# Moving the gate projections of five token tiles from a branch-B unit to the branch-A unit after it

## The chip, the cores and the metric

The kernel runs on one core of one Trainium2 chip. The metric is the device time of one launch in microseconds (us). Before the change three runs took 2355.49 to 2356.97 us, with a median of 2356.01. Engines are called by the profile's names: PE is TensorE, DVE is VectorE, ACT is ScalarE, POOL is GpSimd, and SP is SyncE, which issues nearly all DMAs.

## What is computed

One layer of a streaming encoder: 2048 prompt tokens, and 8 running streams with 16 new tokens each and a cache of 512. The parts that matter here:

```
h = rms_norm(x, norm_g) * (1 + scale) + shift
qa, ka, va, za, qb, kb, vb, zb, ga, gb = split(h @ w_in)
# branch A: 4 heads, two softmaxes each, chunk-causal
w = softmax(q1 k1) - lam * softmax(q2 k2);  oa = w @ v
# branch B: 8 heads, stick-breaking, causal
a = sigmoid(z) * prod over later keys of sigmoid(-z);  ob = a @ v
ya = (norm(oa) * silu(za)) @ w_branch_a;  yb = (ob * silu(zb)) @ w_branch_b
y = x + gate * ((sigmoid(ga) * ya + sigmoid(gb) * yb) @ w_out)
```

The change is about `ga` and `gb`, each 1024 columns wide: the gates. They are projected from h like q, k and v, but nothing reads them before the last stage of the kernel.

## The kernel before

**Tiles and units.** Tokens go in 17 tiles of 128: prompt tiles 0 to 15, and tile NT = 16 with the 8 x 16 new tokens of the running streams. Attention goes in 8 units. Unit u = 2h is head h of branch A, unit u = 2h + 1 is a pair of heads of branch B. Values that need more than 16 bits are held as two float16 parts, so that a projection of 1024 input rows is 8 x 3 = 24 matmuls (high by high, high by low, low by high) of up to 512 columns.

**Projections.** `project(U, t)` (L406) makes q, k, v and z of one unit for one tile: 12 pieces of two matmuls each (L427) into one bank of PSUM ("mm"), then evictions, rotation and stores. For units with a gate width, 12 more pieces follow (`gate_piece`, L487): 24 matmuls of 512 columns (L494) into the one bank "t" from the same tile of h, an eviction with a scale on ACT (L497) into one half of the buffer gts, and a store to `g_d` in memory (L498). `GATES` (L58) gives the units their columns: branch-A units have width 0, each of the four branch-B units has 512 of the 2048 gate columns. So all 17 tiles' gates of a branch-B unit are projected in the same step as its q, k, v and z.

**Weights.** `prepare_unit(u)` (L307) loads the weights of a unit, takes their norm, and cuts them into float16 parts, in buffers from the list `free`: 4 buffers for q, k, v and z, and 4 more for the gates of a branch-B unit. It begins in the attention step of tile NT of the unit before (for unit 1: of tile 3), and is spread over the following steps. `begin` (L842) gives all buffers of the unit before back to the list when the projections of the next unit start.

**The order of the work.** All projection pieces stand in one list, `line`, in order of steps (u, t), t = NT, 0, 1, ..., 15. The transposes of q and k of a step (`transpose_qk`, L502), also through bank "t", follow behind piece 5 of the next step. The outer loop goes through the steps' attention: scores (L629, L630, and the mask L633), then for branch A the row maximum with the eviction (L548), exponentials (L119), sums and weights (L586 to L593), and for branch B two sigmoids (L119), a scan along the keys (L606), a product on POOL (L612) and the float16 parts (L562, L563); DMA turns the weights into `wt` (L570); two steps later come the products with v (L677 to L679, L681 and L682). At each attention step `take` (L878) takes projection pieces from the line up to `position(len(steps) * past / whole + LEAD)`, where `past` is a planned duration of the attention so far (`duration`, L888) and LEAD is 5 steps. So projections run five tiles ahead at the start of a unit, and the first five tiles of a unit are projected beside the last attention tiles of the unit before. `interleave` (L91) mixes these pieces evenly among the score pieces and the products with v; a scheduler then settles each engine's order. Each engine works through its own queue in that order.

**The last stage** (from L1250) reads `g_d`, z and the attention's output tile by tile, makes the branch products, and with them the output; the cached streams' attention is done beside it.

Of the kernel before, what the change touches and what calls it, by code (L numbers as in the profile page):

```python
# [20 lines left out]
AF = mybir.ActivationFunctionType  # L21
# [6 lines left out]
KT = D // P  # L28
# [4 lines left out]
NT = SEQ // P  # L33
# [22 lines left out]
SAMPLE_TIME = 0.3  # L56

GATES = [(u // 2 * 512, u % 2 * 512) for u in range(8)]  # L58

C_ROPE = 0  # L60
C_ID = C_ROPE + 17 * 96
# [48 lines left out]
def layer_kernel(ctx: ExitStack, tc: tile.TileContext, a: dict):  # L110
    nc = tc.nc
    V, S, G, T = nc.vector, nc.scalar, nc.gpsimd, nc.tensor
# [61 lines left out]
    def buffers_of_4k(name, n):  # L174
        pool = ctx.enter_context(tc.tile_pool(name=name, bufs=1, side="right", reuse_waits="tile"))
        return [pool.tile([P, 1024], F32, name=f"{name}{i}") for i in range(n)]


    free = buffers_of_4k("wa", 8)
# [7 lines left out]
    def bank(tag, dt=F32):  # L187
        return ps.tile([P, 512 if dt == F32 else 1024], dt, tag=tag, name=f"ps_{tag}", bufs=BANKS[tag])
# [19 lines left out]
    def total(col, n=1):  # L208

        p = bank("t")  # L210
        T.matmul(p[:, 0:n], ones, col, start=True, stop=True)
        return p[:, 0:n]

    def scales(square, pool, name, n=1):

        tag = "sc" if n == 1 else f"sc{n}"
        kw = {} if n == 1 else dict(bufs=1)
        q = tiny.tile([P, n], F32, tag=tag + "_q", name="sc_q", **kw)
        V.tensor_scalar(out=q, in0=square, scalar1=2.0 ** -46, scalar2=None, op0=ALU.max)
        f = tiny.tile([P, n], I32, tag=tag + "_f", name="sc_f", **kw)  # L220
        V.tensor_scalar(out=f, in0=q.bitcast(I32), scalar1=24, scalar2=None, op0=ALU.logical_shift_right)
        e = tiny.tile([P, 2 * n], I32, tag=tag + "_e", name="sc_e", **kw)
        V.tensor_scalar(out=e[:, 0:n], in0=f, scalar1=-1.0, scalar2=204.0, op0=ALU.mult, op1=ALU.add)
        V.tensor_scalar(out=e[:, n : 2 * n], in0=f, scalar1=50.0, scalar2=None, op0=ALU.add)
        s = pool.tile([P, 2 * n], I32, tag=name, name=name)
        V.tensor_scalar(out=s, in0=e, scalar1=23, scalar2=None, op0=ALU.logical_shift_left)
        return s.bitcast(F32)
# [39 lines left out]
    def sum_squares(src, n, dst, width=1024, scale=1.0):  # L267

        for i in range(0, n, width):
            junk = tiny.tile([P, width], F16, tag="junk", name="junk", bufs=1)  # L270
            w = min(width, n - i)
            S.activation(out=junk[:, 0:w], in_=src[:, i : i + w], func=AF.Square, scale=scale,  # L272
                         accum_out=dst[:, i // width : i // width + 1])

    def add_up(acc, n):
        if n == 1:
            return acc[:, 0:1]
        col = tiny.tile([P, 1], F32, tag="col", name="col")
        V.tensor_reduce(out=col, in_=acc[:, 0:n], axis=AX.X, op=ALU.add)
        return col  # L280
# [6 lines left out]
    def split(hi, lo, src, s, on=None):  # L287

        if on is S:
            S.activation(out=hi, in_=src, func=AF.Identity, scale=s)  # L290
        elif on is G:
            G.tensor_scalar(out=hi, in0=src, scalar1=s, scalar2=0.0, op0=ALU.mult, op1=ALU.add)
        else:
            V.tensor_scalar(out=hi, in0=src, scalar1=s, scalar2=None, op0=ALU.mult)
        V.scalar_tensor_tensor(out=lo, in0=src, scalar=s, in1=hi, op0=ALU.mult, op1=ALU.subtract)
# [8 lines left out]
    sh_box = []  # L304
    units = [None] * 8

    def prepare_unit(u, keep=None):  # L307


        h, kind = u // 2, u % 2  # L310
        U = dict(h=h, kind=kind, u=u, w=[], wg=[], bufs=[])
        units[u] = U
        raw = {}
        g0, gw = GATES[u]
        gk = 1024 // gw if gw else 0

        def fetch(name, k):
            raw[name, k] = b = free.pop(0) if keep is None else keep[:, k // 2, :]
            if name == "w":
                st = b.rearrange("p (k j n) -> p k j n", k=2, n=P)  # L320
                for i in range(2):
                    load(out=st[:, i, :, :], in_=w_in[:, k + i, :].rearrange("p (j n) -> p j n", n=512)[:, 4 * kind : 4 * kind + 4, h * P : (h + 1) * P])
            else:
                load(out=b.rearrange("p (k n) -> p k n", k=gk), in_=w_in[:, k : k + gk, 4096 + g0 : 4096 + g0 + gw])

        def norm(name, k, i):
            if k == 0:
                U[name + "acc"] = unit.tile([P, 4], F32, tag=name + "acc", name=name + "acc")
            fetch(name, k)
            sum_squares(raw[name, k], 1024, U[name + "acc"][:, i : i + 1])  # L330

        def bounds():
            fsq = total(add_up(U["wacc"], 4))
            U["sw"] = scales(fsq, unit, "sw")
            U["fsq"] = unit.tile([P, 1], F32, tag="fsq", name="fsq")
            V.tensor_copy(out=U["fsq"], in_=fsq)

        def bounds_g():
            U["sg"] = scales(total(add_up(U["gacc"], KT // gk)), unit, "sg")

        def split_to(name, k):

            b = free.pop(0)
            U["bufs"].append(b)
            if keep is None:
                free.append(raw[name, k])
            return raw[name, k], b.bitcast(F16)

        def cut(k):
            st, w = split_to("w", k)  # L350
            for i in range(2):
                x = w.rearrange("p (i f n) -> p i f n", i=2, f=2)[:, i, :, :]
                split(x[:, 0, :], x[:, 1, :], st[:, i * 512 : (i + 1) * 512], U["sw"][:, 0:1], S if i % 2 else G)
                U["w"].append(x)

        def gate_cut(k):
            st, w = split_to("g", k)
            w = w.rearrange("p (k f n) -> p k f n", k=gk, f=2)
            split(w[:, :, 0, :], w[:, :, 1, :], st.rearrange("p (k n) -> p k n", k=gk), U["sg"][:, 0:1], S if k else G)
            U["wg"].append(w)  # L360

        pieces = [lambda k=k: norm("w", k, k // 2) for k in range(0, KT, 2)] + [bounds] + [lambda k=k: cut(k) for k in range(0, KT, 2)]
        if gw:
            pieces += [lambda k=k: norm("g", k, k // gk) for k in range(0, KT, gk)] + [bounds_g] + [lambda k=k: gate_cut(k) for k in range(0, KT, gk)]
        return pieces
# [35 lines left out]
    def fetch_h(u, t):  # L401
        ahead[u, t] = hs[len(fetched) % 3].bitcast(F16).rearrange("p (f k n) -> p f k n", f=2, n=P)
        fetched.append(t)
        load(out=ahead[u, t], in_=hT_d[t // 4][:, t % 4, :, :, :])

    def project(U, t):  # L406

        kind, h, sc, sq = U["kind"], U["h"], U["sc"], U["sq"]
        g, i = t // 4, t % 4
        box = {}  # L410
# [70 lines left out]
                load(out=s_d[U["u"]][:, 6:8, :], in_=vt.rearrange("p c f d -> p c (f d)"))  # L481
            U["q16", t], U["k16", t] = qb, k16

        g0, gw = GATES[U["u"]]
        per = 1024 // gw if gw else 0

        def gate_piece(n):  # L487

            if n == 0:
                box["g"] = bank("t")  # L490
            for j in range(per * n, per * n + per):
                hi, wi = ((0, 0), (0, 1), (1, 0))[j % 3]
                k = j // 3
                T.matmul(box["g"][:, 0:gw], box["h"][:, hi, k, :], U["wg"][k // per][:, k % per, wi, :], start=(j == 0), stop=(j == 3 * KT - 1))  # L494
            if per * n + per == 3 * KT:
                gt = gts[:, t % 2 * 512 : t % 2 * 512 + 512]
                S.activation(out=gt[:, 0:gw], in_=box["g"][:, 0:gw], func=AF.Identity, scale=sc[:, 6:7])  # L497
                load(out=g_d[t][:, g0 : g0 + gw], in_=gt[:, 0:gw])  # L498

        return [lambda n=n: piece(n) for n in range(12)] + [lambda n=n: gate_piece(n) for n in range(3 * KT // per if gw else 0)]  # L500

    def transpose_qk(U, t):  # L502
# [339 lines left out]
    def begin(u, t):  # L842
        if t == NT:
            if u > 0:
                free.extend(units[u - 1]["bufs"])
            finish_unit(u)

    def projection(m):
        u, t = steps[m]
        made = []  # L850

        def piece(i):
            if i == 0:
                begin(u, t)
                made.extend(project(units[u], t))
            if i == H_AT and not at_hand and m + 1 < len(steps) and steps[m + 1] not in ahead:
                fetch_h(*steps[m + 1])
            made[i]()

        return [lambda i=i: piece(i) for i in range(12 + 3 * GATES[u][1] // 128)]  # L860

    starts = []
    for m in range(len(steps)):
# [359 lines left out]
    for n in range(len(steps) + PV_LAG):  # L1223
        made, qk, vs = [], [], []
        if n < len(steps):
            u, t = steps[n]
# [174 lines left out]
```

## Time and profile before

| | us |
|---|---|
| median of 3 runs | 2356.01 |
| the profiled execution | 2354.99 |
| its span | 2353.2 |
| PE busy | 2125.0 |
| DVE busy | 1734.5 |
| ACT busy | 1600.0 |
| POOL busy | 726.2 |

The span is the time from the first to the last instruction in the profile; some 1.8 us of the execution lie around it. Busy time is that in which an engine has at least one instruction under way. The units' attention runs from about 120 us to about 1790 us, the last stage from there to the end. In the rows of the view by stretches, each engine's busy time is followed by the number of its instructions, and then come PE's granted clock (1.00 is full speed), the busy share of the 16 DMA engines and what they moved. A row of waits gives who waited for whom, the total in us, how many times, and the longest.

### The profile page before, as it was taken

The numbers are of one execution on the slowest core, as the hardware profiler recorded it, in microseconds if no ns is written. First come the engines' busy times: TensorE is split into PE (matmuls) and PEld (weight loads), VectorE is DVE, ScalarE is ACT, GpSimd is POOL, SyncE is SP. The second block draws the span as 40 slices with busy tenths as digits, with TensorE's granted clock in tenths as the row PEclk, the third lists the DMA queues.
The fourth block names the chain that finished last, engine by engine and source line by source line (L and its number), as shares of the span: only waits on it lengthen the run. The fifth ranks groups of instructions, "written<-read, shape, count | busy, mean of one in ns | idle before, by whom it ended". The sixth has DMA issues, their size and how long they took to land. (4 is left out here: it accounts for less than half of the span.)

```text
span 2353.2 us, 42526 instructions
## 1 busy us (share of the span) xinstructions
PE 2125.0 (90%) x15272; PEld 1146.4 (49%) x15272; DVE 1734.5 (74%) x3604; ACT 1600.0 (68%) x3116; POOL 726.2 (31%) x595
## 2 busy tenths in 40 slices
PE   5898898998999999899999989999995788889998
PEld 3554454444555445445545544554553344444553
DVE  4848766779775667988667798777778777887764
ACT  4557778777786777778677787866777455555651
POOL 1533012345400233641023364103335333332221
PEclk7999999999999999999999999999996999999999
DMA  9766659888795898878577787866687999999531
GB/s 333 250 205 178 160 134 254 192 196 160 188 237 135 197 224 194 168 183 202 135 186 194 177 186 181 197 150 158 152 180 174 273 259 260 249 232 259 167 100 54
DMA packets 843571, 453.73 MB, mean 193 GB/s; under 512 B 538234, under 2 KB 786346, under 8 KB 842848
## 3 DMA queue, kind: packets, MB, share of 16 engines
q1 hardware_dynamic: 842412, 450.63, 77.4%
q8 instruction: 119, 1.95, 0.3%
q14 instruction: 92, 0.75, 0.1%
q10 hardware_dynamic: 948, 0.39, 0.1%
HBM read 249.80 MB, written 73.44 MB: 137 GB/s over the span
## 5 line engine op out<-in xcount | busy, mean ns | idle before, releaser
L612 POOL TENSOR_TENSOR sc_p<-sc_p,sc_n 128x127 f32<-128x127 f32 (+7 forms) x192 | 310.9, 1623 | 887.9 <-DVE sc_n L606 868.9
L427 PE MATMUL ps_mm<-wb,hs 128*128 128x512 f16 x1632 | 413.9, 381 | 6.2 <-DMA hs<-hT_d 6.0
L427 PEld LDWEIGHTS <-hs 128*128 128x128 f16 x3120 | 272.8, 98 | 251.2 <-DMA hs<-hT_d 8.9
L427 PE MATMUL ps_mm<-wa,hs 128*128 128x512 f16 x1488 | 374.2, 382 | 3.7 <-DVE nm L576 2.4
L606 DVE TENSOR_TENSOR_SCAN sc_n<-ps_s,sc_n,zero_t 128x512 f32<-128x512 f32 x192 | 245.3, 1278 | 76.9 <-ACT ps_s L119 73.6
L629 PE MATMUL ps_s<-k,qst 128*128 128x512 f16 (+3 forms) x640 | 226.8, 355 | 45.6 <-DVE sc_n L606 34.7
L563 DVE TENSOR_TENSOR sc_n<-sc_p,sc_n 128x128 f16<-128x128 f32 (+7 forms) x192 | 221.5, 1158 | 50.0 <-ACT sc_n L562 49.7
L494 PEld LDWEIGHTS <-hs 128*128 128x128 f16 x1632 | 155.1, 98 | 183.9 <-DVE qst L522 8.4
L119 ACT ACTIVATE sc_p<-ps_s,usc 128x512 f32<-128x512 f32 (+3 forms) x320 | 203.4, 636 | 46.3 <-PE ps_s L630 35.0
L630 PE MATMUL ps_s<-k,qst 128*128 128x512 f16 (+3 forms) x640 | 226.7, 355 | 0.0
L681 PE MATMUL ps_o<-v,wt 128*128 128x128 f16 x1088 | 175.7, 227 | 34.5 <-DMA wt<-sc_n 34.2
L494 PE MATMUL ps_t<-wb,hs 128*128 128x512 f16 x816 | 193.1, 381 | 7.3 <-DVE qst L522 7.2
L562 ACT CAST sc_n<-sc_p 128x128 f16<-128x128 f32 (+7 forms) x192 | 154.6, 808 | 65.7 <-POOL sc_p L612 65.2
L119 ACT ACTIVATE ps_s<-ps_s,usc 128x512 f32<-128x512 f32 (+3 forms) x328 | 198.4, 605 | 0.0
L494 PE MATMUL ps_t<-wa,hs 128*128 128x512 f16 x816 | 193.2, 381 | 1.9 <-ACT qst L522 1.7
L1318 PE MATMUL ps_o<-wo,wb 128*128 128x512 f16 x816 | 188.2, 385 | 0.7 <-ACT wb L1142 0.7
L682 PE MATMUL ps_o<-v,wt 128*128 128x64 f16 x1088 | 160.6, 199 | 0.0
L681 PEld LDWEIGHTS <-wt 128*128 128x128 f16 x1088 | 106.7, 102 | 102.4 <-DMA wt<-sc_n 46.4
L606 DVE TENSOR_TENSOR_SCAN sc_n<-ps_s,zero_t 128x128 f32<-128x128 f32 (+3 forms) x128 | 104.3, 815 | 48.6 <-ACT ps_s L119 46.5
L548 DVE TENSOR_SCALAR_CACHE_REDUCE sc_p<-ps_s,usc 128x512 f32<-128x512 f32 (+3 forms) x160 | 106.2, 664 | 37.9 <-PE ps_s L630 24.0
L682 PEld LDWEIGHTS <-wt 128*128 128x128 f16 x1088 | 104.2, 101 | 56.2 <-issue 1.6
L548 DVE TENSOR_SCALAR_CACHE_REDUCE sc_n<-ps_s,usc 128x512 f32<-128x512 f32 (+3 forms) x160 | 106.3, 665 | 29.9 <-PE ps_s L630 17.2
(345 smaller groups left out, 4483.4 us busy)
## 6 DMA issues: line engine op xcount, KB each, us to landing
hs<-hT_d SPq DMA_DIRECT2D x130, 512.0 KB, 4.5
g_d<-gt SPq DMA_DIRECT2D x68, 256.0 KB, 4.3
wb<-g_d SPq DMA_DIRECT2D x26, 512.0 KB, 5.8
out_dram<-pr SPq DMA_DIRECT2D x204, 64.0 KB, 2.1
z_d<-pr SPq DMA_DIRECT2D x136, 64.0 KB, 1.8
o_d<-o SPq DMA_DIRECT2D x136, 64.0 KB, 2.3
hs<-z_d SPq DMA_DIRECT2D x17, 512.0 KB, 4.5
hs<-o_d SPq DMA_DIRECT2D x17, 512.0 KB, 5.0
```

What stands on the lines that cost most here:

```text
L119: i = S.activation(**kw)
L427: T.matmul(box["p"], box["h"][:, hi, k, :], U["w"][k][:, wi, :], start=(n == 0), stop=(n == 3 * KT - 1))
L494: T.matmul(box["g"][:, 0:gw], box["h"][:, hi, k, :], U["wg"][k // per][:, k % per, wi, :], start=(j == 0), stop=(j == 3 * KT - 1))
L548: V.tensor_scalar(out=dst[:, lo : lo + n], in0=p[:, 0:n], scalar1=sc_pos, scalar2=None, op0=ALU.mult, op1=ALU.max, accum_out=job["mx"][:, ...
L563: V.tensor_tensor(out=lo, in0=src, in1=hi, op=ALU.subtract)
L606: V.tensor_tensor_scan(out=dst[:, lo : lo + n][:, ::-1], data0=src[:, 0:n][:, ::-1], data1=zero_t[:, 0:1].to_broadcast([P, n]), initial=fi ...
L612: G.tensor_tensor(out=p[:, 0:m], in0=p[:, 0:m], in1=n[:, 1 : m + 1], op=ALU.mult)
L629: T.matmul(p[:, 0:n], qst[:, c, :], kk[:, c, 0:n], start=True, stop=False)
L630: T.matmul(p[:, 0:n], qst[:, 2 + c, :], kk[:, c, 0:n], start=False, stop=not diag)
L681: T.matmul(po[:, c * P : (c + 1) * P], wt[:, wj, :], vt[:, c, :, :], start=first, stop=False)
L682: T.matmul(po[:, c * P : c * P + 64], wt[:, nb + wj, :], vt[:, c, 0, :], start=False, stop=last)
L1318: T.matmul(po, st["y"][:, yi * 8 + k, :], wo[j * 4 + k // 2][:, wi, k % 2, :], start=(n == 0), stop=(n == 3 * KT - 1))
```

## The change

The gates of tiles NT, 0, 1, 2 and 3 of units 1, 3 and 5 are projected one unit later: in the step of the same tile of unit 2, 4 or 6, from the tile of h that this step has loaded. The weights are those that were prepared with unit 1, 3 or 5. Unit 7 has no unit behind it and keeps all its gates. The four gate buffers are given back when the last of the five tiles is done. The steps of the line get 24 or 12 pieces accordingly; when each step is taken stays the same.

```diff
+GATES_LATER = [NT, 0, 1, 2, 3]
...
+    def gates_of(u, t):
+
+        if u % 2 == 0:
+            return u - 1 if u > 0 and t in GATES_LATER else None
+        return None if u < 7 and t in GATES_LATER else u
...
-        g0, gw = GATES[U["u"]]
+        ug = gates_of(U["u"], t)
+        g0, gw = GATES[ug] if ug is not None else (0, 0)
...
-                T.matmul(box["g"][:, 0:gw], box["h"][:, hi, k, :], U["wg"][k // per][:, k % per, wi, :], start=(j == 0), stop=(j == 3 * KT - 1))
+                T.matmul(box["g"][:, 0:gw], box["h"][:, hi, k, :], units[ug]["wg"][k // per][:, k % per, wi, :], start=(j == 0), stop=(j == 3 * KT - 1))
...
-                S.activation(out=gt[:, 0:gw], in_=box["g"][:, 0:gw], func=AF.Identity, scale=sc[:, 6:7])
+                S.activation(out=gt[:, 0:gw], in_=box["g"][:, 0:gw], func=AF.Identity, scale=units[ug]["sc"][:, 6:7])
+                if ug < U["u"] and t == GATES_LATER[-1]:
+                    free.extend(units[ug]["bufs"][4:])
...
-                free.extend(units[u - 1]["bufs"])
+                free.extend(units[u - 1]["bufs"][0:4])
...
-        return [lambda i=i: piece(i) for i in range(12 + 3 * GATES[u][1] // 128)]
+        return [lambda i=i: piece(i) for i in range(12 if gates_of(u, t) is None else 24)]
```

## The prediction

> **What bounds the kernel now.** I read the page first, for the shares and the clock, then the busy time by stretches of time, and then the waits of single stretches.
>
> ```profile
> PE 2125.0 (90%) x15272; PEld 1146.4 (49%) x15272; DVE 1734.5 (74%) x3604; ACT 1600.0 (68%) x3116; POOL 726.2 (31%) x595
> ...
> PEclk7999999999999999999999999999996999999999
> ```
>
> TensorE is busy for 90% of the span, so it is the engine to look at, but the 10% left are what the change plays with: it moves TensorE work in time and takes none away. So the question is where the idle tenths lie. The source view of the gate matmuls (L494) has a row that shows where they stand, in 40 slices of 58.8 us:
>
> ```profile
> busy tenths in 40 slices 0000567850038677001787700177870000000000
> ```
>
> The four humps are the gates of units 1, 3, 5 and 7. Each begins before its unit's attention does, at about 250, 685, 1108 and 1517 us: projections run some five tiles ahead of attention, so the gates of the first five tiles (t = NT, 0, 1, 2, 3) stand beside the last attention tiles of the branch-A unit before. The zeros between humps begin with the last attention tiles of the branch-B unit, beside which the next unit, of branch A, is projected without any gate. I call the first kind of stretch A-end and the second B-end. The change carries five tiles of gates from three A-ends to the three B-ends behind them. This is the view by stretches:
>
> ```profile
> core 0: us, PE busy (x) PEld busy (x) DVE busy (x) ACT busy (x) POOL busy (x), PEclk, DMA share, GB/s
> 252.00:325.00 73.00, 71.66 (x536) 40.75 (x537) 50.07 (x131) 54.18 (x107) 0.00 (x0) 1.00 0.75 177
> 685.00:752.00 67.00, 66.23 (x462) 36.10 (x460) 41.91 (x106) 44.81 (x87) 0.00 (x0) 1.00 0.70 162
> 1108.00:1174.00 66.00, 66.00 (x459) 36.14 (x456) 43.77 (x110) 42.03 (x81) 0.00 (x0) 1.00 0.61 138
> 500.00:562.00 62.00, 52.90 (x455) 30.15 (x454) 57.38 (x69) 54.41 (x101) 40.49 (x27) 1.00 0.94 191
> 928.00:992.00 64.00, 53.97 (x442) 29.63 (x441) 61.29 (x68) 52.35 (x97) 39.91 (x27) 1.00 0.85 184
> 1342.00:1403.00 61.00, 51.03 (x436) 28.96 (x435) 57.81 (x64) 51.17 (x94) 40.22 (x27) 1.00 0.90 198
> 562.00:595.00 33.00, 27.32 (x200) 14.94 (x197) 28.98 (x75) 21.82 (x55) 12.93 (x15) 0.95 0.65 146
> 992.00:1026.00 34.00, 29.78 (x222) 16.73 (x221) 29.79 (x81) 25.75 (x65) 15.90 (x18) 0.95 0.68 157
> 1403.00:1433.00 30.00, 26.79 (x212) 14.59 (x210) 27.70 (x72) 20.14 (x49) 15.46 (x15) 1.00 0.69 153
> 200.00:252.00 52.00, 40.34 (x278) 22.99 (x276) 47.18 (x137) 42.43 (x98) 12.61 (x15) 0.87 0.66 170
> 776.00:851.00 75.00, 66.66 (x391) 33.01 (x390) 43.67 (x82) 55.63 (x112) 18.57 (x13) 0.93 0.93 232
> 865.00:935.00 70.00, 69.14 (x473) 36.27 (x472) 51.68 (x76) 52.48 (x99) 24.57 (x16) 1.00 0.80 188
> 1044.00:1108.00 64.00, 62.04 (x456) 34.70 (x455) 53.31 (x147) 54.35 (x130) 15.00 (x18) 1.00 0.87 211
> ```
>
> The first three rows are the A-ends: PE busy 98 to 100% of 206 us in all, DVE only 63 to 69%, ACT 64 to 74%. The next three are the B-ends: DVE busy 93 to 96% of 187 us in all, PE 84%. So the gates are carried from where TensorE sets the time to where VectorE sets it. The waits inside these stretches say the same; first VectorE's in the three A-ends, then TensorE's in the three B-ends:
>
> ```profile
> DVE l L586 <- ACT sc_n L119: 8.7, 3, 5.6
> ...
> DVE l L586 <- ACT sc_n L119: 11.7, 3, 4.6
> ...
> DVE l L586 <- ACT sc_n L119: 12.2, 3, 4.6
> ```
>
> ```profile
> PE ps_s L629 <- DVE sc_n L606: 6.6, 11, 1.5
> ...
> PE ps_s L629 <- DVE sc_n L606: 7.1, 9, 1.6
> ...
> PE ps_s L629 <- DVE sc_n L606: 7.9, 8, 1.9
> ```
>
> **The change part by part.** No instruction is added or dropped; each engine's count stays. What moves is 3 units times 5 tiles: 15 groups of 24 matmuls, 15 evictions on ACT (L497), 15 stores to g_d. The price of one group is in the time line, from its start to the start of the next matmul:
>
> ```profile
> 301.15 5.34 PE L494 MATMUL ps_t<-wa,hs 128*128 128x512 f16 x24
> 306.33 1.03 PE L427 MATMUL ps_mm<-wb,hs 128*128 128x512 f16 x4
> ```
>
> 306.33 - 301.15 = 5.18 us, or 0.216 us a matmul. Five groups are 25.9 us for a unit, 77.7 us for the three.
>
> *Taken from the A-ends.* With 25.9 us less, PE has 45.8, 40.3 and 40.1 us left there. ACT loses 5 x 0.687 us (row below) = 3.4 us and has 50.8, 41.4 and 38.6; DVE keeps 50.1, 41.9 and 43.8. The stretches can't be shorter than the busiest of these: 50.8, 41.9, 43.8, together 136.5 against 206: a saving of at most 69.5 us. At the other end, DVE keeps the stall that it has now for the exponentials on ACT: 50.1 + 8.7, 41.9 + 11.7 and 43.8 + 12.2 make 168.4, a saving of 37.6 us. What is late next is thus DVE, behind it the chain from row maximum to exponentials to weights. The nearest row for attention of branch A that DVE bounds is 200 to 252 us, with neither gates nor many projections: DVE 47.18 of 52, or 91%. At 91% the A-ends take 55.2, 46.2 and 48.3 us, a saving of 56. I take 50 us, between 37.6 and 56 and nearer to the row that shows the engine's share than to a stall that was measured with TensorE as the bound.
>
> *Added to the B-ends.* PE idles 62 - 52.90 = 9.1, 10.0 and 10.0 us there, 29.1 together. 77.7 us of gates fill that and lengthen the stretches by 48.6 us, if PE is then busy all the time. The first tiles of the following A unit still run off VectorE's backlog: DVE 88, 88 and 92% of the rows at 562, 992 and 1403 us, PE idle 5.7, 4.2 and 3.2 us. A longer B-end lets DVE work that backlog off earlier, so up to 13.1 us can come back: the cost is 35.5 to 48.6 us. Would PE be busy all the time? The row at 865 us is the same branch with gates of every tile: PE 69.14 of 70, DVE at 75% of PE's time and ACT at 76%. In the B-ends PE would have 78.8, 79.9 and 76.9 us, with DVE at 73, 77 and 75% of that: the same mix. I take 40 us.
>
> *Sum:* -50 + 40 = **-10 us**, small beside its terms. The profiled execution took 2354.99 us with a span of 2353.2, so 2345 us; the median before, 2356.01, is 1.0 above it, so **2346 us**.
>
> *What goes with the matmuls.* In the changed order, the gate groups stand in PE's queue where they block score matmuls of branch B in place of those of branch A. Rows for the other resources that a group touches:
>
> ```profile
> L497 ACT ACTIVATE gt<-ps_t,usc x68: 666/687/752, 263.9 to 1751.8; 128x512 f32<-128x512 f32 x68
> ...
>   PE ps_t L507: 2.9, 5
> ```
>
> ```profile
> PE ps_t L494 <- DVE qst L522: 7.4, 5, 3.2
> ...
> PE ps_mm L427 <- DMA hs<-hT_d: 7.1, 5, 2.4
> ```
>
> ```profile
> g_d<-gt SPq DMA_DIRECT2D x68, 256.0 KB, 4.3
> ```
>
> The one PSUM bank "t" is shared by transposes and gates. In all 68 groups PE lost 2.9 us to the eviction and 7.4 us to the copies before a gate; 15 of 68 of that is 2.3 us. In the B-ends the copies run on ACT, which is at 82 to 88% there, so I expect 0 to 5 us in all, inside the range. The evictions, 3.4 us on ACT for a unit, lie beside PE's 78. Each h tile is read longer by its unit A step and shorter by its unit B step; PE's whole wait for h is 7.1 us, so this is nothing or 2 us either way. On SP 15 stores of 256 KB pass from queues with a DMA share of 0.61 to 0.75 to those at 0.85 to 0.94. That share falls as the B-ends lengthen (0.90 of 61 us is 55 us, of 77 us it is 0.71), so I cost it at nothing; if that cover is missing, weights turned by DMA land late, the slower rival below. The four weight buffers that each B unit keeps for five more tiles are given back just as the next B unit's preparation begins, which takes the buffers ahead of them in the list first; nothing waits. Unit 7 keeps its gates, so the A-end at 1517 us stays as it is.
>
> **The clock.** TensorE's granted clock falls where it idles:
>
> ```profile
> 220.00:230.00 10.00, 7.25 (x75) 4.96 (x73) 9.85 (x26) 9.50 (x28) 3.63 (x5) 0.87 0.80 251
> 230.00:240.00 10.00, 6.08 (x30) 2.93 (x28) 10.00 (x32) 10.00 (x24) 3.04 (x3) 0.79 0.24 68
> 240.00:252.00 12.00, 7.01 (x51) 4.61 (x50) 11.97 (x30) 9.38 (x24) 0.00 (x0) 0.72 0.45 87
> 988.00:998.00 10.00, 7.79 (x69) 5.15 (x67) 9.73 (x15) 5.18 (x10) 6.95 (x5) 0.87 0.76 154
> ```
>
> At 61 to 78% busy in ten microseconds it was 0.72 to 0.87; the B-ends, at 84% as a whole, held 1.00. The relieved A-ends would have PE at 126.2 of 156 us, 81%, on the edge. If they got 0.87, PE's 126.2 us would take 18.9 us more, part of it under DVE. The Trainium skill has a rule that speaks against the change here: in "TensorE: Matmul & The Clock Gate", Part 1, it says that after an idle window of about 3.4 us the array goes back to half rate. By the rule the moved matmuls keep B-ends fast and put A-ends at risk; this trace agrees so far that the low rows are those with the emptiest PE.
>
> **The rivals.**
> - *A bigger gain.* The A-ends come near the busiest engine's time (a saving of 56 to 69.5) and the backlog comes back in full (a cost of 35.5): -20.5 to -34 us, 2322 to 2335.5. For it: DVE at 98 to 100% in the rows from 220 to 252 us. Against it: ACT and DVE are almost equal in the A-ends and wait for each other.
> - *No gain: the chain holds.* The A-ends keep the stall for the exponentials, a saving of 37.6, and B-ends cost 40: +2.4 us, 2358.4. For it: the stall is there three times in each A-end. Against it: where no gates are projected, from 1044 to 1108 us, DVE is busy 83% beside a PE at 97%.
> - *No gain: the clock.* A-ends at 0.87 give back up to 18.9 us, half of it under DVE: about -10 + 9.5, 2355.5 us.
> - *Slower: the B-ends do not fill.* In-order TensorE then waits now for scans, now for turned weights, now for the bank, as it did at 776 to 851 us, in a stretch of branch B with gates: PE 66.66 of 75, 89%, with a DMA share of 0.93. At 89% the B-ends take 78.8 / 0.889 = 88.6, 89.8 and 86.5 us, 78 us more than now; with 50 saved that is +28, 2384 us. The point from which it decides: a cost above 50 us, which is PE under 235.6 / 237 = 99% in the B-ends if none of the 13.1 us comes back, and under 94% (235.6 / 250) if all of it does. For it: B-ends have the highest DMA shares. Against it: the row at 865 us, 99% with the same mix of engines.
>
> **How the numbers follow.** Forecast -10 us: 0.50, with its own range of 2336 to 2353. Bigger gain: 0.14. The chain holds: 0.13. The clock: 0.05. The B-ends don't fill: 0.18. The range is 2326 to 2366: it leaves out the far part of the bigger gain (0.04) and most of the slow rival (0.14). A difference within 0.2%, 4.7 us, is about what a measurement of this kernel can't tell from none. Faster by more than that: 0.44 of the forecast's 0.50 and 0.14, 0.58. Within: 0.06, and 0.10 and 0.03 of the two rivals without gain, 0.19. Slower: 0.03, 0.02 and 0.18, 0.23.
>
> **What would show each step.** In the changed profile the humps of L494 should begin about 50 to 70 us later for the first three units, and not for the fourth. The three A-ends (attention of the last three A tiles and the first B tile) should be 15 to 19 us shorter each, with DVE near 90% and PE under 90%; the B-ends 12 to 16 us longer each, with PE at 98% or more and the wait of L629 for the scan L606 gone. Wrong would be: A-ends with PE idle and the wait of L586 for ACT as long as now; a clock under 0.95 in them; B-ends with PE under 94%, waiting for turned weights (wt), for L606 or for the bank "t"; or a difference elsewhere, above all after 1800 us, where nothing but buffer names and some order changes.

## The result and the profile after

The changed kernel took 2371.49 us (median of 4 runs, 2369.12 to 2375.52) against 2355.75 for the kernel before (4 runs): a ratio of 1.0073, 95% interval 1.006 to 1.0086. It is slower by 15.7 us, where 10 us less were forecast. The profiled execution took 2369.12 us, with a span of 2367.2, 14.0 above before's. Its page and the source view of the gate matmuls (now L503), where the humps for units 1, 3 and 5 begin one slice later and the fourth one stays:

```profile
PE 2133.3 (90%) x15272; PEld 1150.6 (49%) x15272; DVE 1730.1 (73%) x3604; ACT 1600.4 (68%) x3116; POOL 713.8 (30%) x595
```

```profile
busy tenths in 40 slices 0000037883002697500189750277780000000000
```

To compare stretches that hold the same attention, I bound them by mask matmuls (L633 before, L644 after; two a unit and tile, the start of the second): an A-end from tile 11 of an A unit to tile 3 of the B unit behind it, a B-end from tile 12 of a B unit to tile 3 of the A unit behind it, and unit 7 from the last tile of unit 6 to its own. The view by stretches of the kernel before: three A-ends, three B-ends, unit 7; columns as in the prediction.

```profile
249.00:345.00 96.00, 90.90 (x685) 51.84 (x684) 63.33 (x156) 73.11 (x155) 3.81 (x6) 1.00 0.72 167
665.00:771.00 106.00, 100.65 (x725) 56.37 (x724) 66.69 (x165) 75.43 (x160) 6.40 (x9) 0.98 0.75 171
1094.00:1192.00 98.00, 97.37 (x699) 54.20 (x698) 64.77 (x162) 68.77 (x145) 4.67 (x7) 1.00 0.65 147
489.00:579.00 90.00, 77.56 (x627) 43.50 (x626) 79.32 (x113) 72.77 (x141) 52.99 (x39) 0.98 0.88 183
916.00:1013.00 97.00, 82.39 (x659) 45.72 (x658) 86.67 (x120) 76.21 (x149) 54.64 (x40) 0.98 0.82 184
1331.00:1421.00 90.00, 77.62 (x650) 43.80 (x648) 82.44 (x116) 70.68 (x136) 54.75 (x39) 1.00 0.87 191
1574.00:1791.00 217.00, 197.94 (x1406) 107.10 (x1404) 165.97 (x265) 157.24 (x299) 78.50 (x51) 0.96 0.71 162
```

The same seven of the changed kernel:

```profile
248.00:326.00 78.00, 70.78 (x557) 42.09 (x556) 59.83 (x152) 67.31 (x145) 3.92 (x5) 0.96 0.73 171
670.00:758.00 88.00, 79.29 (x615) 47.66 (x613) 66.81 (x168) 69.07 (x149) 7.93 (x9) 0.96 0.79 182
1097.00:1177.00 80.00, 74.92 (x585) 43.40 (x584) 63.61 (x162) 61.43 (x135) 5.52 (x7) 1.00 0.73 160
477.00:584.00 107.00, 101.78 (x761) 55.33 (x760) 79.88 (x125) 78.30 (x151) 46.93 (x37) 0.98 0.88 190
903.00:1006.00 103.00, 100.08 (x761) 54.49 (x759) 79.02 (x125) 77.10 (x147) 47.78 (x37) 1.00 0.87 190
1318.00:1419.00 101.00, 99.11 (x753) 54.00 (x751) 77.17 (x122) 73.65 (x139) 47.45 (x37) 1.00 0.84 189
1575.00:1808.00 233.00, 205.09 (x1426) 109.11 (x1424) 174.71 (x262) 157.31 (x298) 79.73 (x51) 0.93 0.66 150
```

With the exact starts, the A-ends give -18.3, -17.2 and -17.6 = **-53.1 us** (forecast -50), the B-ends +17.2, +6.1 and +11.7 = **+35.0** (forecast +40). Unit 7, in which no gate was moved, is 232.6 us long in place of 216.5: **+16.2**. What is left of the spans' 14.0 us is 14.0 + 53.1 - 35.0 - 16.2 = +16.0. Nearly all of that remainder lies in two places, the middle of unit 1 (+6.8) and of unit 4 (+10.1), that is, between the two bounded ends. Their rows, before and then after:

```profile
345.00:489.00 144.00, 134.42 (x862) 68.19 (x861) 96.97 (x163) 107.35 (x207) 45.38 (x31) 0.99 0.89 208
1013.00:1094.00 81.00, 79.42 (x561) 43.69 (x559) 68.13 (x195) 67.16 (x160) 25.29 (x31) 1.00 0.81 200
```

```profile
326.00:477.00 151.00, 135.55 (x872) 69.89 (x871) 105.88 (x166) 109.19 (x213) 45.94 (x32) 0.95 0.79 187
1006.00:1097.00 91.00, 85.50 (x585) 46.24 (x583) 67.08 (x190) 71.06 (x169) 29.52 (x34) 0.98 0.77 188
```

Unit 4's middle holds 6.1 us more of PE's work, 24 matmuls more (x561 to x585). This is work put off from the B-end just before it: that B-end (the one at 916 us before, at 903 after) holds only 102 matmuls more (x659 to x761), where five groups of gates are 120, because it holds 16 projection matmuls fewer, and unit 4's middle holds 20 more. Counted with this middle, the three B-ends took +45.1 us, and the two terms together gave about -8, near the forecast of -10. Unit 1's middle holds 1.1 us more of PE's work and lasts 7 us longer, at a lower clock (0.95 in place of 0.99).

TensorE's waits in the whole kernel say the same. Before (total us, times, longest), then after:

```profile
PE ps_s L629 <- DVE sc_n L606: 34.7, 41, 2.0
PE ps_o L681 <- DMA wt<-sc_n: 34.2, 24, 4.6
PE ps_o L677 <- DMA wt<-sc_n: 18.0, 15, 3.1
```

```profile
PE ps_o L692 <- DMA wt<-sc_n: 39.6, 31, 3.7
PE ps_o L688 <- DMA wt<-sc_n: 29.4, 22, 3.3
PE ps_mm L435 <- DMA hs<-hT_d: 24.1, 12, 6.7
PE ps_s L640 <- DVE sc_n L617: 19.5, 21, 3.7
PE ps_t L518 <- ACT gt L506: 6.7, 8, 2.6
```

The wait for scans fell by 15.2 us (in the three B-ends from 21.6 to 1.0), as forecast. Waits for turned weights rose by 16.8 (34.2 + 18.0 to 39.6 + 29.4), and those for tiles of h by 17.0, from the 7.1 that the prediction quotes to 24.1. Of these 24.1, 9.7 lie in unit 7 (1.5 before). Another 7.5 lie in the middle of unit 3, which is 1.2 us shorter all the same, with 24 projection matmuls fewer. One of the waits in unit 7, in TensorE's and then in SyncE's time line:

```profile
1655.22 1.46 PE L503 MATMUL ps_t<-wb,hs 128*128 128x512 f16 x6
...
1658.68 0.38 PE L435 MATMUL ps_mm<-wa,hs 128*128 128x512 f16 x1
1660.89 1.90 PE L435 MATMUL ps_mm<-wb,hs 128*128 128x512 f16 x8 [1.82 <-DMA hs<-hT_d]
```

```profile
1656.71 0.32 SPq L412 DMA_DIRECT2D hs<-hT_d  x1
1657.43 0.32 SPq L509 DMA_DIRECT2D g_d<-gt  x1
```

The gate's last matmuls end at 1656.68; 0.03 us later SyncE issues the load of the next tile of h, which had been waiting for the buffer; 4.18 us later TensorE goes on with the projection that reads it, after 1.82 us of nothing. SyncE's own waits for gates in unit 7 rose, from before to after (total us, times, longest):

```profile
SPq L404 <- PE ps_t L494: 11.8, 5, 5.6
```

```profile
SPq L412 <- PE ps_t L503: 22.3, 7, 4.8
```

There are three buffers `hs`, in a ring: the load for step m + 3 waits for the last reader of step m, which is a gate.

Why should that be worse in a unit that was not edited? Because the scheduler settles each queue's order for the kernel as a whole. Matching the two kernels' lists of TensorE's instructions without the gates, 4040 of 13389 stand in another relative order. (The figure depends on how one counts: in the two traces, matched by source line, the fewest that would have to be moved are 3308 of 13640.) In unit 7, count the projections of later steps that stand ahead of the first gate matmul of each of the 17 steps: before, it is two for five steps in a row and else one or none; after, two for eleven steps, nine of them in a row. A gate that is two projections late gives its buffer up only when the third projection, which needs that buffer, is already due.

### The profile page after: what moved, and what is told of

The parts are those of the page before. It is cut to its first block, busy times and chain, and to the rows that moved or that the text cites. A ratio compares the mean times of both kernels' runs of the same rounds, so it can differ in the third digit from the quotient of the medians.

```text
span 2367.2 us, 42579 instructions
## 1 busy us (share of the span) xinstructions
PE 2133.3 (90%) x15272; PEld 1150.6 (49%) x15272; DVE 1730.1 (73%) x3604; ACT 1600.4 (68%) x3116; POOL 713.8 (30%) x595
## 5 line engine op out<-in xcount | busy, mean ns | idle before, releaser
L435 PEld LDWEIGHTS <-hs 128*128 128x128 f16 x3120 | 283.9, 99 | 308.3 <-DMA hs<-hT_d 25.5
L435 PE MATMUL ps_mm<-wa,hs 128*128 128x512 f16 x1590 | 393.4, 383 | 13.9 <-DMA hs<-hT_d 11.5
L435 PE MATMUL ps_mm<-wb,hs 128*128 128x512 f16 x1530 | 384.4, 385 | 12.8 <-DMA hs<-hT_d 12.6
L574 DVE TENSOR_TENSOR sc_n<-sc_p,sc_n 128x128 f16<-128x128 f32 (+7 forms) x192 | 216.1, 1131 | 57.3 <-ACT sc_n L573 56.6
L503 PEld LDWEIGHTS <-hs 128*128 128x128 f16 x1632 | 152.3, 98 | 169.8 <-issue 5.4
L692 PE MATMUL ps_o<-v,wt 128*128 128x128 f16 x1088 | 164.4, 225 | 39.8 <-DMA wt<-sc_n 39.6
L503 PE MATMUL ps_t<-wb,hs 128*128 128x512 f16 x816 | 195.9, 383 | 2.8 <-DVE qst L533 2.1
L503 PE MATMUL ps_t<-wa,hs 128*128 128x512 f16 x816 | 193.7, 379 | 1.3 <-DVE qst L533 0.8
L692 PEld LDWEIGHTS <-wt 128*128 128x128 f16 x1088 | 104.4, 101 | 97.6 <-DMA wt<-sc_n 50.3
L693 PE MATMUL ps_o<-v,wt 128*128 128x64 f16 x1088 | 150.7, 198 | 0.0
L468 POOL TENSOR_TENSOR rot<-pr,rope 128x256 f32<-128x256 f32 x68 | 62.0, 911 | 252.0 <-ACT pr L449 190.3
L688 PE MATMUL ps_o<-v,wt 128*128 128x128 f16 x544 | 104.3, 226 | 29.4 <-DMA wt<-sc_n 29.4
```

Source lines behind the costliest of these rows:

```text
L435: T.matmul(box["p"], box["h"][:, hi, k, :], U["w"][k][:, wi, :], start=(n == 0), stop=(n == 3 * KT - 1))
L503: T.matmul(box["g"][:, 0:gw], box["h"][:, hi, k, :], units[ug]["wg"][k // per][:, k % per, wi, :], start=(j == 0), stop=(j == 3 * KT - 1))
L574: V.tensor_tensor(out=lo, in0=src, in1=hi, op=ALU.subtract)
L692: T.matmul(po[:, c * P : (c + 1) * P], wt[:, wj, :], vt[:, c, :, :], start=first, stop=False)
L693: T.matmul(po[:, c * P : c * P + 64], wt[:, nb + wj, :], vt[:, c, 0, :], start=False, stop=last)
```

## The experiments

Theory: the two terms are right, and the loss is made elsewhere, by the order that came out: late gates hold the ring of h. Rivals: the move itself costs more than it brings, whatever the order; or the order of everything else moves the time by as much as the change does. Ratios are to the kernel before on the same chip (its medians were 2355.8 to 2360.9), with 95% intervals.

**One unit alone.** `GATED_LATER` limits the move to unit 1, or to unit 5.

```diff
...
+GATED_LATER = (1,)
...
-            return u - 1 if u > 0 and t in GATES_LATER else None
+            return u - 1 if u - 1 in GATED_LATER and t in GATES_LATER else None
...
```

> Gates of the five tiles moved for unit 1 alone. Theory A (the move itself pays, what was lost is that late gates hold the three h buffers, above all in unit 7): 5 to 10 us faster than before (2346 to 2351 us), unit 7's attention as long as before (216 us), TensorE's waits for h tiles under 10 us in all. Theory B (what is moved costs more in its new place than in its old one, a third of the loss for each unit): 5 us slower, 2361 us, spread over units 1 and 2.

> Gates of the five tiles moved for unit 5 alone. In the order of this program unit 7's gates stand two projections behind their tile for nine tiles in a row, as in the full change; with unit 1 alone they stand as before. Theory A: unit 7's attention takes 226 to 233 us instead of 216, with some 10 us of waits for h tiles, and the whole is 3 to 12 us slower (2359 to 2368). Theory B: 5 us slower with unit 7 as long as before, the loss in units 5 and 6.

Unit 1 alone: 2366.01 us, 1.0045 (1.0023 to 1.0066): slower, where theory A gave 5 to 10 us less. By size and place it is nearer to theory B, 5 us more over units 1 and 2. Attention is 10.9 us ahead at the end of unit 0 and 1.7 at that of unit 1, as the terms say, but 10.6 behind at the end of unit 2, from which nothing was moved; unit 7 lasts 217.1. Unit 5 alone: 2371.03 us, 1.0051 (1.0036 to 1.0065). Every unit up to 3 ends within 0.5 us of before, unit 4 ends 9.9 early, unit 5 0.5 late, unit 6 0.3 late, and unit 7 17.9 late, with 12.5 us of waits for h in it. So five gates at one pair of ends are worth about nothing, and the loss lies behind them, in two different places.

**A fourth buffer for h.** It takes the place of one of the 16 weight buffers, so that in unit 7 one weight less can be prepared ahead for the last stage; both kernels.

```diff
...
-        ahead[u, t] = hs[len(fetched) % 3].bitcast(F16)...
+        ahead[u, t] = hs[len(fetched) % len(hs)].bitcast(F16)...
...
-    free += buffers_of_4k("wb", 8)
+    free += buffers_of_4k("wb", 7)
+    hs += buffers_of_4k("hx", 1)
...
```

> The full change with a fourth buffer for h tiles, its room taken from one of the sixteen weight buffers (the list of free buffers gets 15; in unit 7 one branch weight less is cut early). Theory A: waits for h tiles fall from 24 us to under 6, and it is 10 to 25 us faster than the same kernel without the move (h4 of before). Theory B: waits for h fall, the time stays within 5 us of the full change, 2366 to 2376.

> The kernel before with the same fourth h buffer and 15 weight buffers: the control. Theory A: waits for h go from 7 us to about 0, time 2347 to 2357. Theory B: 2353 to 2358.

After: 2348.25 us, 0.9958 (0.9942 to 0.9973), faster than both kernels. Before: 2368.6, 1.004 (1.0026 to 1.0055), above what either theory gave (2347 to 2358). With four buffers the move gains 20 us, with three it loses 16. But the order changed from the start too, so this difference does not show the cause. What tells more is unit 7 of the changed kernel: gates stand two late for nine steps in a row as with three buffers, nothing there waits for h, and it is the shortest of all:

```profile
1571.00:1784.00 213.00, 197.75 (x1422) 107.18 (x1419) 169.60 (x264) 155.19 (x297) 79.11 (x51) 0.96 0.72 163
```

**No gate late, in all units.** An order without a semaphore: the first matmul of a projection stands behind the last gate matmul of two steps before.

```diff
...
+            if n == 0 and len(box_ends) > 1 and box_ends[-2] is not None:
+                tc.add_manual_dep(i.ins, box_ends[-2].ins.name, NOSYNC, reason="gate order")
...
```

> The full change, with each projection's first matmul kept in TensorE's order behind the gate of the tile two steps before, so that no gate stands more than one projection behind its tile; buffers and work unchanged. Theory C (the loss is the ring of three h buffers: a gate two projections late holds the buffer that the next load needs): waits for h tiles fall from 26 us to under 9, unit 7's attention from 233 to 215 to 222 us, the time by 10 to 20 us to 2351 to 2361. Rival D (the ring is one of many stalls that the new order deals out; others take its place): waits for h fall, but waits for bank t and turned weights rise by as much, and the time falls by less than 5 us.

> The kernel before with the same rule for the order, as a control. Theory C: waits for h were only 8 us, so at most 8 us are gained, 2350 to 2358. Rival D: anything within 10 us either way of before, since the order changes.

After: 2366.62 us, 1.0039 (1.0021 to 1.0057); before: 2361.87, 1.0021 (1.0012 to 1.003). No wait for h is left in either, and the changed kernel's unit 7 falls to 219.8, yet the ratio only goes from 1.0073 to 1.0039, less than the 10 to 20 us of theory C. In the profiled execution (2374.18 us, 7.6 above the median) unit 6 already ends 15.2 us later than before. A rule for all units changes too much at once to settle the question.

**Order alone.** LEAD 5.1 in place of 5.0; nothing else.

> The kernel before with the lead of the projections set to 5.1 steps in place of 5.0: one or two pieces of projection stand earlier, nothing else. It measures what a change of order alone does. Theory C: within 4 us of before. Rival D: 5 to 15 us away from before, either way.

> The full change with a lead of 5.1 steps. Its gates stand two projections late for nine tiles of unit 7, as in the full change. Theory C: unit 7 again loses 10 to 16 us with waits for h, 2365 to 2378 in all. Rival D: 5 to 15 us away from the full change, either way.

Before: 2366.93 us, 1.0043 (1.003 to 1.0057); after: 2385.83, 1.0121 (1.0106 to 1.0137). A change that moves no gate from unit to unit costs the kernel before 0.43%; counted in the traces as above, it leaves 3495 of TensorE's 13640 other matmuls in another order, about as many as the change does. It costs them in the same place: unit 7 of the kernel before lasts 234.8 us with LEAD 5.1, in place of 216.5, with 4 us more of PE's work. But TensorE never waits for h there. It waits for turned weights; its row in unit 7 with LEAD 5.0, then with 5.1:

```profile
PE ps_o L681 <- DMA wt<-sc_n: 6.0, 5, 2.7
```

```profile
PE ps_o L681 <- DMA wt<-sc_n: 24.6, 10, 7.6
```

So a long unit 7 is not by itself the mark of the ring of h: the order can stall it by another transfer too. In the changed kernel with LEAD 5.1 unit 7 lasts 254.5 us, with 12.7 us of waits for h and 19.1 for turned weights; theory C gave 2365 to 2378 us for that kernel. An effect of a few tenths of a per cent can't be read here from one pair of kernels.

**The order as written.** `schedule_with_timeline_sim=False`, both kernels.

> The kernel before, with its instructions in the order in which the program writes them (the reordering by simulated times switched off), on every engine; no work is added or taken away. No theory gives its own time: what counts is the pair with the next run. All that is said here: the order alone is worth more than 10 us (1.2% and more off the kernel before, in either direction), if the theory is right that the order of everything that was not moved weighs as much as the move. If it is within 5 us of the kernel before, that theory is weak.

> The changed kernel in the order in which it is written. Against the run before it, few instructions but the gates' stand otherwise (1565 of 13389 of PE's, where the pair as given has 4040). Theory 'order': the move itself is worth its two terms (about -50 us at the ends of branch A, about +35 to +40 at the ends of branch B), and what made the changed kernel slower was the order that came out around it: 10 to 25 us faster than the run before it, and no wait of projections for hT. Rival 'the move itself': work beside it is pushed, whatever the order: 5 to 16 us slower than the run before it.

Before: 2578.48 us, 1.0923 (1.0904 to 1.0942); after: 2591.23, 1.0969 (1.095 to 1.0987). The move costs 12.7 us here, and I had expected a gain: the rival holds in this order. Exact stretches: A-ends -23.2, -16.1, -21.6 = -60.9, B-ends +25.5, +25.0, +24.5 = +75.0, against 25.9 us of gates each. The B-ends' idle time took up nothing. TensorE's waits in the whole kernel, before and after:

```profile
PE ps_t L507 <- DVE k L295: 63.8, 40, 4.8
...
PE ps_t L507 <- ACT gt L497: 43.6, 23, 3.7
PE ps_s L629 <- DVE sc_n L606: 40.9, 29, 3.3
```

```profile
PE ps_t L518 <- ACT gt L506: 68.5, 35, 3.7
...
PE ps_t L518 <- DVE k L297: 34.6, 35, 4.4
PE ps_s L640 <- DVE sc_n L617: 22.6, 17, 3.5
```

What was no longer lost to copies of k (-29.2) and scans (-18.3) was lost to evictions of gates (+24.9) and elsewhere. Whether gates fill idle time depends here on their places in the queue, not on the idle time alone.

**Fewer gates, and unit 5 left out.** `GATES_LATER = [NT, 0]`, and `GATED_LATER = (1, 3)` with all five tiles.

> The changed kernel with only two token tiles' gates of each unit moved (the register tile's and the first's), six in all in place of fifteen: 6 x 5.18 = 31 us of gates. In unit 7 the gates stand among the projections as in the kernel before. Theory 'hT ring': what was lost lay in unit 7, by loads of hT that came late; here unit 7 lasts 216 us as before, projections wait for hT under 10 us in all, and the two terms (-20 and +12 to +16) leave 2348 to 2356. Theory 'order': the same two terms, but anything between 2340 and 2370, with the difference to the kernel before made in units 1 to 6 where no gate was moved from or to.

> The changed kernel, with the gates of units 1 and 3 moved and those of unit 5 left where they were. Unit 7's gates stand as in the kernel before. Theory 'hT ring': two thirds of the terms (-33 and +23) and none of the loss in unit 7: 2343 to 2350, unit 7 at 216 us. Theory 'order': no loss in unit 7 either, but 2345 to 2370, by stretches of units 2, 3 and 5 where no work was moved.

Two tiles: 2351.94 us, 0.9956 (0.994 to 0.9972), faster, by as much as order alone can make. Units 1 and 3: 2369.05, 1.0033 (1.0018 to 1.0049). Unit 7 was kept as it was in both (217.5 and 217.6 us), as the theory of h says, but the second did not get the 2343 to 2350 that it gave. Its loss looks the same in another place: unit 5, which kept all its gates, has them two late in nine steps (in one step before), lasts 240.7 us in place of 227.1, and TensorE waits there:

```profile
PE ps_mm L436 <- DMA hs<-hT_d: 11.8, 6, 3.6
```

The kernel before has no such row in its unit 5. At most five of these nine steps stand in a row, and so do five in unit 7 of the kernel before, where the wait was 1.5 us. The count of late gates alone thus does not give the size of the loss.

**The rule in unit 7 alone, three tiles, and two with four buffers for h.** Up to unit 7's first projections, each engine's order is that of the kernel without the rule. The other two are `GATES_LATER = [NT, 0, 1]`, and [NT, 0] with the edit for the fourth buffer.

```diff
...
+            if U["u"] == 7 and n == 0 and box_ends[-2] is not None:
+                tc.add_manual_dep(i.ins, box_ends[-2].ins.name, NOSYNC, reason="gate order")
...
```

> The changed kernel, with one rule more for the order, in unit 7 alone: the first matmul of a projection there stands behind the last gate matmul of two steps before, so that no gate is more than one projection late. Up to unit 7 every engine's order is that of the changed kernel. Theory 'hT ring': unit 7 lasts 214 to 222 us in place of 232.6, projections no longer wait for hT there, and the whole is 10 to 17 us faster than the changed kernel: 2354 to 2362. Rival 'loss by something else in unit 7' (weights coming late, the clock, transposes of scores): unit 7 stays at 228 us or above, the whole at 2366 or above.

> The gates of unit 5 alone moved, and the same rule in unit 7. Up to unit 4 the order is the kernel before's, and units 6 and 7 ended level with it but for the loss in unit 7 (17.9 us). Theory 'hT ring': 2350 to 2358, as the kernel before or a few us faster; unit 7 at 214 to 222 us. Rival: unit 7 at 230 us or above, 2366 to 2372 as without the rule.

> Three token tiles' gates of each unit moved, nine in all (46.6 us). Unit 7's order is the kernel before's. Theory 'room at the end of branch B': with two per unit the ends of A gave -36 and the ends of B took 8.5 of 31 us; with five they gave -53 and took 35. The third gate costs more than the first two: the ends of B take +14 to +20 here, the whole is 2348 to 2358, between the run with two and the kernel before. Rival 'order alone': no such row; anything between 2340 and 2372, with the ends of B under +10 or over +25.

> Two token tiles' gates moved, and a fourth hT tile in place of one of sixteen weight buffers. Theory 'hT ring': with two gates moved the projections waited only 10 us for hT, so the fourth tile is worth 5 to 10 us here: 2340 to 2348, the best of all. Rival 'order alone': the fourth tile slowed the kernel before by 9 us and sped the changed one by 23, by the order that came out; here anything from 2335 to 2370.

The changed kernel with the rule: 2359.93 us, 1.0004 (0.9991 to 1.0018). Unit 5 alone with it: 2354.06, 0.9977 (0.9967 to 0.9987), against 1.0051 without. Unit 7, first of the changed kernel with the rule, then of unit 5 alone without and with it:

```profile
1577.00:1798.00 221.00, 200.94 (x1408) 107.64 (x1407) 169.40 (x267) 156.30 (x299) 76.81 (x51) 0.94 0.69 158
```

```profile
1574.00:1809.00 235.00, 206.33 (x1428) 109.24 (x1427) 176.31 (x262) 157.35 (x299) 80.68 (x51) 0.93 0.65 149
```

```profile
1574.00:1796.00 222.00, 201.00 (x1409) 107.73 (x1407) 169.26 (x267) 156.68 (x299) 77.36 (x51) 0.95 0.70 157
```

By the mask matmuls, 232.6 to 221.0 and 234.0 to 222.0, with no wait for h left there. The theory holds for some 12 us; the last 5 stay open. With the same order up to unit 7, the profiled executions of the changed kernel with and without the rule stand up to 5.9 us apart at the end of a unit, so a single stretch of one execution may be off by that much. And with unit 7's loss nearly out, the changed kernel is level with the one before, not 10 us ahead.

Three tiles: 2340.71 us, **0.9923** (0.991 to 0.9935), the fastest of all, and better than the 2348 to 2358 that I expected. Its ends of A give -16.2, -17.5, -14.9 = -48.5, its ends of B take +8.4, -1.2, +5.7 = +12.9 of 46.6 us of gates, and unit 7 lasts 217.3. Two tiles with the fourth buffer: 2357.82, 0.9994 (0.9984 to 1.0004), where 2340 to 2348 was expected. Where few waits for h were left, the fourth buffer brought nothing. Its ends of A gave only 11.3 us, in place of 36.2; that the order it came with made this difference is argued, not shown.

**Four tiles.** `GATES_LATER = [NT, 0, 1, 2]`, without and with the rule in unit 7.

> Four token tiles' gates of each unit moved, twelve in all. In unit 7 the gates of tiles 6 to 12 stand two projections late in the order. Theory 'hT ring': unit 7 lasts 224 to 234 us, projections wait for hT there; theory 'room': the ends of A give -50, the ends of B take +20 to +28. Together 2350 to 2364. Rival 'order alone': unit 7 within 3 us of 216.5, or a whole outside 2345 to 2368.

> The same, with the rule in unit 7 alone that no gate is more than one projection late. Theory 'hT ring': unit 7 at 215 to 222 us and 6 to 15 us faster than the run before it. Rival 'loss by something else': unit 7 within 3 us of the run before it, and the whole too.

Without: 2363.95 us, 1.0033 (1.0021 to 1.0045), in the expected range, though the ends of B took 38.2 us and not the 20 to 28 that were part of it. With: 2347.61, 0.9972 (0.996 to 0.9984), 16.3 us faster. Unit 7's waits of TensorE for h and its rows:

```profile
PE ps_mm L435 <- DMA hs<-hT_d: 10.0, 6, 4.5
```

```profile
1573.00:1801.00 228.00, 201.30 (x1410) 107.36 (x1407) 169.77 (x262) 154.77 (x297) 78.39 (x51) 0.95 0.69 152
```

```profile
1572.00:1788.00 216.00, 198.34 (x1404) 107.21 (x1402) 166.96 (x263) 156.99 (x299) 75.74 (x50) 0.96 0.72 161
```

The first two are the kernel without the rule: 10.0 us of waits, unit 7 227.7 us long. With the rule there is no such wait, and it is 216.6. All of what was lost there is back.

The points by number of tiles, in us, from mask matmuls; "rest" is what is left of the span's difference:

| tiles moved | gates moved | A-ends | B-ends | unit 7 | rest | ratio |
|---|---|---|---|---|---|---|
| 2 | 31.1 | -36.2 | +8.5 | +1.1 | +23.0 | 0.9956 |
| 3 | 46.6 | -48.5 | +12.9 | +0.8 | +20.2 | 0.9923 |
| 4 | 62.2 | -44.9 | +38.2 | +11.2 | +4.6 | 1.0033 |
| 5 | 77.7 | -53.1 | +35.0 | +16.2 | +16.0 | 1.0073 |

The A-ends give no more, beyond a few us, after three tiles; the B-ends take three cheaply, and 22 to 25 us more with four or five. "Rest" holds work that passed from the ends to the middles. With two and three tiles the A-ends lose more than the gates moved (36.2 of 31.1 us, 48.5 of 46.6), so other work left them too. In all four, unit 4's middle is longer: counted with it, the B-ends took 14.5, 21.4, 40.7 and 45.1 us. The step behind three tiles stays, at 19 to 24 us. Each row is one order of one kernel, so its single entries are not to be read to the us.

## Why the prediction was wrong

- **The move and its price** held: PE's busy time is 63.9 us less in the A-ends (20.1, 21.4 and 22.4) and 63.4 more in the B-ends. All 77.7 us of gates lie inside these bounds: each A-end goes from 144 gate matmuls to 24, each B-end from 24 to 144. Part of the difference is other work that moved against them: the A-ends hold 56 projection matmuls more, some 12 us, and the B-ends 23 fewer.
- **-50 and +40** held in size: -53.1, and +35.0 (+45.1 with the work put off into unit 4's middle). In the B-ends PE is busy 95, 97 and 98%, and the wait for scans there is nearly gone, as said. The ground for -50 did not hold: in the A-ends DVE is at 76 to 80%, not at 91, and PE still leads with 90 to 94%. So that size was reckoned from a limit that did not come, and that it fits is in part luck.
- **The clock** is 0.96, 0.96 and 1.00 in the A-ends, not 0.87, so that rival is out. (Of the rows that the prediction sums up as 61 to 78% busy, the one at 240 us is 58% busy.) The Trainium skill says in "TensorE: Matmul & The Clock Gate", Part 1, that the array drops to half rate after an idle window of about 3.4 us. The trace neither bears this out nor speaks against it: the longest waits of TensorE in the three A-ends, 3.7, 2.8 and 2.1 us, went with these three clocks.
- **The step that failed** is "Each h tile is read longer by its unit A step and shorter by its unit B step; PE's whole wait for h is 7.1 us, so this is nothing or 2 us either way". The wait rose to 24.1 us. I priced the time for which a buffer is read, and not the ring behind it: with three buffers, slack for two late projections is about nil, so a run of late gates can stop TensorE at one step after another. The runs show this for unit 7. The loss goes out with the rule (about 12 us in two kernels, 11 in a third). It is out with a fourth buffer at the same lateness, and absent where unit 7's gates stood as before (two and three tiles). It seems to come again in unit 5 where that one's gates came late (units 1 and 3 moved, +13.6 us, with 11.8 us of waits for h). It makes some 12 of the 25.7 us between -10 and +15.7; the rest is under "Open".
- **Under it lay an assumption** not even written down as one: "Unit 7 keeps its gates, so the A-end at 1517 us stays as it is". Its gates stayed in their unit, but not at their places in the queue. The order of 4040 other instructions moved with the edit, and order alone (LEAD 5.1) is worth 0.43%, made in unit 7 with no wait for h. The prediction named "a difference elsewhere" as what would make it wrong, and gave it no chance of its own.
- **Turned weights** were costed at nothing because the DMA share in the B-ends would fall to 0.71. It stayed at 0.88, 0.87 and 0.84, and waits for them rose by 16.8 us. No run isolated that; with LEAD 5.1 alone they rose by 18.6 us in unit 7.
- **The rivals.** "The B-ends do not fill" had the right sign for another reason: they fill in the changed kernel. They do not in the order as written, where the move costs 12.7 us. "The chain holds" is out: VectorE's wait for the exponentials (L586, now L597) fell from 33.9 to 14.8 us in the three A-ends.
- **Open:** 4.6 and 5.6 us of unit 7 that the rule left in two kernels; the 10.6 us behind after unit 2 with unit 1 alone, where theory B's time was the nearer one; and which of order, clock and turned weights made unit 1's middle 6.8 us longer. By the start of unit 7 the changed kernel is 1.0 us late in place of the 10 gained; of these 11 us, 2 are the two terms' and 6.8 the middle of unit 1. That the order made the rest, or the whole, is not shown.

## What to carry to other kernels

Before pricing a moved step, list the buffers that it reads last, and ask how late it may stand before the ring behind them stops the engine. Where a scheduler orders the queues, compare the whole order, and the stages that were not edited first; order alone moved this kernel by 0.4%, so take several variants before believing a difference of that size. And move by portions: here the B-ends took the gates of three tiles for little and those of a fourth for 19 us more, and the version with three tiles beats the one with five by 1.5% (0.9923 against 1.0073). With unit 7's stall out of the latter it is 0.8% (0.9923 against 1.0004), of which order alone could make about half.

## What the runs showed of the hardware

- A load of one tile of h (512 KB) took 4.18 us from SyncE's issue to the matmul that needed it. Issued 0.03 us after its buffer came free, it still cost TensorE 1.82 us: other work covered 2.4.
- Taking the waits for h out of unit 7 gave back about as much as they were: 11.6 us for 9.7 (changed kernel), 12.0 for 12.5 (unit 5 alone) and 11.1 for 10.0 (four tiles).
- In unit 7 of the changed kernel the granted clock was 0.93, in place of 0.96, and 0.94 with these waits gone.
